# A convolution trunk in which two channel tiles of layer 1 change places, with one raw weight tile less and one general tile more

## The chip, the cores and the metric

The kernel runs on one core of a Trainium2 chip. The metric is the device time of one execution in microseconds; the median of three runs is quoted, and a profile of one execution is read beside it. Engines are named as in the profile: PE is the tensor engine, DVE the vector engine, ACT the scalar engine, POOL the GpSimd engine, and SP the queue from which all transfers are issued here.

## The reference

Two layers work on x of 2048 tokens by 1024 channels in float32. Each layer is `x + post_norm(mixer(pre_norm(x)))` with RMS norms. Layer 0 is a mixer of sliding-window attention and causal pooling. Layer 1, where the change lies, is a convolution module:

```
proj = h @ w_in                                  # 1024 x 3072
a, b, gate = split(proj, 3)
glu  = a * sigmoid(b)
conv = causal depthwise convolution of glu, 31 taps, + bias
mu, var = mean and variance of conv over all 1024 channels
cn = (conv - mu) * rsqrt(var + eps) * ln_g + ln_b
y  = silu(cn) * silu(gate)
out = y @ w_out
x  = x + rms_norm(out, post_norm)
```

The mean over all channels is what matters below: no part of `cn` can be formed before the convolution of each channel is there.

## The kernel before

Channels lie on the 128 partitions, so the 1024 channels are 8 tiles, numbered 0 to 7. Tokens are cut into two halves of 1024, and each half into two blocks of 512. A projection is 24 matmuls of 128x512 into one PSUM bank: 8 channel tiles k, and for each of them three matmuls, because every float32 operand is split in a high part and a low part: high weight by high input, high weight by low input, low weight by high input (`project`, L407). A weight tile is loaded raw, 512 KB, into a `wr` tile (`w_load`, L342). Then ACT copies its high part into `wh`, and DVE subtracts to get its low part `wl` (`w_split`, L373). For the weights `wc` of layer 1's input projection, the low part is formed once, kept in DRAM (`wcl`) and loaded from there. The raw tile is given back when both parts are there. The weights of the last block are different in one thing: their high and low parts are kept in general tiles `s4`, because this block is projected in two column parts of 256 (`last_block`, L1038), with matmuls of 128x256; there each weight is used for 24 matmuls and comes back for the second part.

Layer 1 runs in stages. For each half, `inproj1` (L1235) goes through the channel tiles in the order of `CONV_ORDER`; for each tile it projects b and a for both blocks. What comes next depends on the tile. Tiles 0, 1, 3, 5 and 7 are convolved on DVE (`conv_dve`, L1054): 29 multiply-add instructions of 128x1024, two starts and a sum, per half; the result goes to DRAM (`cd`). Tiles 2, 4 and 6 are convolved on PE (`conv_pe`, L1075) for both halves at once, when half 1's values are there: the values go to DRAM (`gt`), come back in another layout, are multiplied by Toeplitz tiles (`in_toep`) into the banks a0 and a1, and the results are stored in DRAM (`ct`) and loaded from there. After half 1's input projection come the gates (`gates1`, 16 projections), and while these run, `norms` (L1188) loads the convolved tiles of half 0, adds them up, takes their mean by a matmul with ones (`a0<-s4,ones`), the variance, and makes the mix: high and low parts for each tile k. Then `outproj` (L974) multiplies half 0's mix by the output weights (`in_wo`, eight projections for each block), and in this time the mix of half 1 is made. Half 1's first block is projected next, and its second block is the last block.

All instructions are issued through one helper, so the profile shows them on L189. The order in which they are issued is that of `Flow` (L54), a planner that runs when the program is built. PE's main line (the projections) goes on, and tasks with a priority (norms, convolutions, loads) are taken whenever, by its own cost estimates, their data are there and DVE and ACT are not more than `LAG` ahead of PE. Each engine then takes its instructions strictly in that order. SP's queue too is in that order. Tiles are taken from pools whose sizes are in `SLOTS` (L41); a task that finds its pool empty is not issued, and another goes ahead of it, so that a pool's size moves the whole order.

Of the kernel before, what the change touches and what calls it, by code (L numbers as in the profile page):

```python
# [34 lines left out]
DVE_CONV = (0, 1, 3, 5, 7)  # L35
PE_CONV = tuple(i for i in range(KT) if i not in DVE_CONV)
POOL_ORDER = (("u", 3), ("g", 3), ("u", 2), ("g", 2), ("u", 1), ("g", 1), ("u", 0), ("g", 0))
CONV_ORDER = (0, 1, 2, 3, 4, 5, 6, 7)

SLOTS = {  # L40
    "s4": 37, "t2": 5, "wr": 3, "wh": 2, "wl": 2, "xh": 2, "xr": 2, "ab": 1, "st": 3, "ms": 3, "rs": 2, "rh": 6,  # L41
    "mm": 4, "a0": 1, "a1": 1, "pt": 1, "pv": 1,
}
PACK = (
# [163 lines left out]
def trunk_kernel(tc, a):  # L208
# [49 lines left out]
    def grab(tag, cols=TH, dt=F32):  # L258
        flow.wait(lambda: avail[tag] > 0)
        return make(tag, cols, dt)  # L260

    def put(*tiles):
        for t in tiles:
            tag = owner.pop(t.name)
            at = 0.0
            for c in range(8):
                k = (t.name, c)
                at = max(at, flow.read.get(k, (0, 0))[0], flow.wrote.get(k, (0, 0))[0])
            freed[tag].append(at)
            freed[tag].sort()  # L270
            avail[tag] += 1
# [40 lines left out]
    wseq = []  # L312
# [2 lines left out]
        wseq += [("wa", 14 + g) if x == "g" else ("wu" if h else "wut", g) for x, g in POOL_ORDER]  # L315
        wseq += [("wo0", f) for b in range(NB) for f in range(KT)]
    for h in range(NH):
        wseq += [("wc", i) for c in CONV_ORDER for i in (8 + c, c)]
        wseq += [("wc", 16 + c) for c in range(KT)]
    for h in range(NH):  # L320
        wseq += [("wo1", f) for b in range(NB) for f in range(KT)]
# [79 lines left out]
    def take(name, i):  # L401
        flow.wait(lambda: wready)
        got = wready.pop(0)
        assert got[:2] == (name, i), (got[:2], name, i)
        return got[2:]

    def project(w, src, b, ready=None, part=slice(0, BL), order=tuple(range(KT)), tag="mm"):  # L407
        wh, wl = w
        bank = grab(tag)
        out = bank[:, :part.stop - part.start]  # L410
        for k in order:
            if ready is not None:
                flow.wait(lambda: ready(k, b))
            hi, lo = (t[:, part] for t in src(k, b))
            T.matmul(out, wh[:, k, :], hi, start=k == order[0], stop=False)
            T.matmul(out, wh[:, k, :], lo, start=False, stop=False)
            T.matmul(out, wl[:, k, :], hi, start=False, stop=k == order[-1])
            flow.pump()
        return bank, flow.t["P"]
# [86 lines left out]
    def pairs(tiles):  # L506
        return lambda k, b: halves(tiles[b][k])
# [604 lines left out]
    def tanh_of(bank, at, ths, b):  # L1112
        yield at
        th = yield from get("t2")
        A.activation(th, bank, AF.Tanh, scale=0.5)
        put(bank)
        ths[b] = th

    def glu(bank, at, ths, b, gv, n):
        yield at  # L1120
        yield from until(lambda: b in ths)
        th = ths[b]
        at = V.scalar_tensor_tensor(
            gv[:, b * PB:(b + 1) * PB, :], th.rearrange("f (p s) -> f p s", p=PB), 1.0,
            bank.rearrange("f (p s) -> f p s", p=PB), op0=ALU.add, op1=ALU.mult)
        put(th, bank)
        n[0] = at
        n[1] += 1

    def after_glu(half, i, gl, n, over):  # L1130
        yield from until(lambda: n[1] == NB)
        yield n[0]
        if i in DVE_CONV:
            slot = DVE_CONV.index(i)
            if half + 1 < NH:
                G.tensor_copy(gc[:, slot, :], gl[:, TH:])
            flow.spawn(conv_dve(half, i, slot, gl, over), 4)
        else:
            view = gt[i].rearrange("r x s -> (r x s)").rearrange("(c q s) -> c q s", c=P, q=PH)
            at = Q.dma_start(out=view[:, :, half * SG:(half + 1) * SG], in_=gl.rearrange("c (q s) -> c q s", q=PH))  # L1140
            put(gl)
            if half + 1 == NH:
                yield at
                flow.spawn(conv_pe(i, over), 2)
# [88 lines left out]
        stored.add((half, j, b))  # L1233

    def inproj1(half, hs, have, over):  # L1235
        for i in CONV_ORDER:
            ths, n = {}, [0.0, 0]
            w = take("wc", 8 + i)
            for b in range(NB):
                flow.spawn(tanh_of(*project(w, pairs(hs), b, lambda k, b: k in have[b]), ths, b), 0)  # L1240
            put(*w)
            dve = i in DVE_CONV
            gl = grab("s4", TH + HIST if dve else TH)
            if dve:
                G.tensor_copy(gl[:, :HIST], gc[:, DVE_CONV.index(i), :])
                gv = gl[:, HIST:].rearrange("f (s p) -> f p s", p=PH)
            else:
                gv = gl.rearrange("f (p s) -> f p s", p=PH)
            w = take("wc", i)
            for b in range(NB):  # L1250
                flow.spawn(glu(*project(w, pairs(hs), b), ths, b, gv, n), 0)
            put(*w)
            flow.spawn(after_glu(half, i, gl, n, over), 1)
# [26 lines left out]
    for half in range(NH):  # L1280
        inproj1(half, hs, have, over)
        now = hs
        hs, have = [{} for _ in range(NB)], [set() for _ in range(NB)]
        if half + 1 < NH:
            flow.spawn(prep(1, half + 1, hs, have, 2), 2)
        else:
            for h in range(NH):
                flow.spawn(norms(h, over, mixes[h], dones[h]), 1)
        gates1(half, now)
# [88 lines left out]
```

## Time and profile before

| what | value |
|---|---|
| median of three runs | 1494.03 us (1493.61 to 1494.33) |
| profiled execution | 1494.47 us |
| its span | 1492.7 us (1.8 us lie around it) |
| PE busy | 1464.9 us (98%), 7226 matmuls |
| DVE busy | 1220.6 us (82%) |
| ACT busy | 587.4 us (39%) |
| chain that ended last | PE 92%, DVE 3%, DMA 3% |

The profile's times start at the span's start. A row of the timeline is a run of like instructions: start, duration, engine, line, operation, out<-in, shape, count, and in brackets the idle time ahead of it with what ended it. Durations of matmuls in a run overlap, so the time of one is read from the distance of the starts. The chain that ended last follows the program back from its last instruction.

In layer 1, half 0's mean is taken at 1211.95 us, half 0's mix is projected from about 1282 us, half 1's mix from 1376.89 us (called X0 below: the first projection of its first block), and the last block from 1430.95 us.

### The profile page before, as it was taken

The page shows a single profiled execution, that of the slowest core. Times are in us where ns is not written, and L with a number is a line of the kernel's source. Part 1 is how long each engine was busy: PE and PEld are TensorE (multiplying, and loading weights), DVE is VectorE, ACT ScalarE, POOL GpSimd, SP SyncE. Part 2 cuts the span into 40 slices and gives each one's busy share as a digit, 9 for nine tenths or more (in the row PEclk, how much of TensorE's full clock was granted, in tenths as well). Part 3 has the DMA queues.
Part 4 walks back from the last instruction along what each step waited for, and adds up shares of the span by engine and source line. Part 5 has one row for each costly group of instructions (what it writes and reads, how often), then busy time and mean ns, then how long its engine had stood idle before and what let it go on. Part 6 is the DMA issues. An engine that isn't in the chain of part 4 may idle for free.

```text
span 1492.7 us, 19290 instructions
## 1 busy us (share of the span) xinstructions
PE 1464.9 (98%) x7226; PEld 1189.9 (80%) x7226; DVE 1220.6 (82%) x1903; ACT 587.4 (39%) x1093; POOL 48.6 (3%) x65
## 2 busy tenths in 40 slices
PE   8999999999999999999999999999999999999896
PEld 6877778788887778788888888888888878878696
DVE  7888877778888787576799999939999699789886
ACT  6454343555454434454211123211212135556541
POOL 0000010000000000000010000000000000000000
PEclk9999999999999999999999999999999999999998
DMA  6122144666551024356632446533654865734685
GB/s 226 60 81 70 66 141 138 197 229 222 187 173 50 29 85 166 106 180 221 202 114 94 132 127 209 186 127 118 214 187 154 273 197 197 242 127 141 213 280 184
DMA packets 121294, 236.78 MB, mean 159 GB/s; under 512 B 33776, under 2 KB 57968, under 8 KB 121200
## 3 DMA queue, kind: packets, MB, share of 16 engines
q1 hardware_dynamic: 121200, 235.55, 48.6%
q8 instruction: 57, 0.93, 0.3%
q14 instruction: 37, 0.30, 0.1%
HBM read 184.13 MB, written 51.38 MB: 158 GB/s over the span
## 4 chain that ended last, share of the span: by engine, by line
PE 92%; DVE 3%; DMA 3%; ACT 1%; issue 0%; SPq 0%; POOL 0%; POOLq 0%; ACTq 0%; DVEq 0%
PE mm L189 81%; PE a L189 5%; PE pv L189 3%; PE pt L189 2%; DVE s L189 2%; DMA s<-in_toep 2%; DMA s<-ct 1%; DVE wl L189 0%; ACT s L189 0%; ACT t L189 0%; DMA wr<-in_wa 0%; DVE t L189 0%; SPq L189 0%; ACT wh L189 0%; DMA ct<-t 0%
## 5 line engine op out<-in xcount | busy, mean ns | idle before, releaser
L189 PE MATMUL mm<-s,wh 128*128 128x512 f32 (+1 forms) x3616 | 1136.1, 395 | 12.4 <-ACT s L189 10.4
L189 PEld LDWEIGHTS mm<-s,wh 128*128 128x128 f32 x3616 | 669.1, 189 | 160.8 <-ACT s L189 11.6
L189 PE MATMUL mm<-s,wl 128*128 128x512 f32 (+1 forms) x1808 | 710.1, 393 | 0.0
L189 PEld LDWEIGHTS mm<-s,wl 128*128 128x128 f32 x1808 | 341.0, 189 | 76.4
L189 DVE SCALAR_TENSOR_TENSOR s<-s,packed,s 128x1024 f32<-128x1024 f32 x290 | 352.6, 1280 | 0.0
L189 ACT ACTIVATE wh<-wr 128x1024 fp32r<-128x1024 f32 (+1 forms) x138 | 145.3, 1053 | 394.1 <-PE mm L189 252.1
L189 DVE TENSOR_TENSOR wl<-wr,wh 128x1024 fp32r<-128x1024 f32 (+1 forms) x90 | 109.1, 1212 | 56.4 <-ACT wh L189 54.9
L189 DVE TENSOR_TENSOR s<-s,s 128x512 f32<-128x512 f32 (+4 forms) x124 | 114.2, 942 | 11.2 <-DMA s<-ct 4.3
L189 ACT ACTIVATE t<-mm 128x512 f32<-128x512 f32 (+1 forms) x122 | 68.6, 562 | 105.5 <-PE mm L189 105.5
L189 DVE TENSOR_TENSOR t<-t,t 128x512 f32<-128x512 f32 (+1 forms) x131 | 86.4, 664 | 16.5 <-ACT t L189 14.5
L189 PE MATMUL a<-s,s 128*128 128x128 f32 (+2 forms) x592 | 91.6, 292 | 3.0 <-DMA s<-in_toep 2.6
L189 PEld LDWEIGHTS a<-s,s 128*128 128x128 f32 x592 | 80.4, 190 | 13.5 <-DMA s<-in_toep 5.6
L189 ACT ACTIVATE s<-mm 128x512 f32<-128x512 f32 (+1 forms) x116 | 67.9, 585 | 52.9 <-PE mm L189 46.8
L189 DVE SCALAR_TENSOR_TENSOR s<-t,mm 128x512 f32<-128x512 f32 x48 | 40.2, 837 | 55.4 <-PE mm L189 51.3
L189 ACT ACTIVATE s<-t 128x512 fp32r<-128x512 f32 (+1 forms) x52 | 48.8, 942 | 53.2 <-DVE t L189 52.6
L189 ACT ACTIVATE t<-s 128x512 f32<-128x512 f32 x80 | 48.6, 628 | 51.2 <-DVE s L189 36.8
L189 DVE TENSOR_TENSOR t<-pt,packed 128x512 f32<-128x512 f32 x64 | 44.1, 689 | 23.6 <-PE pt L189 23.3
L189 DVE TENSOR_TENSOR s<-t,s 128x512 fp32r<-128x512 f32 (+1 forms) x56 | 52.5, 939 | 12.3 <-ACT s L189 11.5
L189 ACT ACTIVATE s<-s 128x512 fp32r<-128x512 f32 (+1 forms) x56 | 44.8, 813 | 32.3 <-DMA s<-in_wc 16.5
L189 ACT ACTIVATE s<-s,st 128x128 f32<-128x128 f32 x128 | 49.4, 388 | 12.2 <-DVE st L189 12.1
L189 POOL TENSOR_TENSOR rs<-ms,mhalf 128x4 f32<-128x4 f32 (+1 forms) x21 | 27.3, 1301 | 796.6 <-DVE ms L189 796.6
L189 DVE TENSOR_TENSOR s<-s,xr 128x512 f32<-128x512 f32 x56 | 37.8, 688 | 8.2 <-DMA xr<-in_xp 5.7
(100 smaller groups left out, 920.0 us busy)
## 6 DMA issues: line engine op xcount, KB each, us to landing
wr<-in_wo SPq DMA_DIRECT2D x64, 512.0 KB, 3.8
wr<-in_wc SPq DMA_DIRECT2D x48, 512.0 KB, 4.8
wl<-wcl SPq DMA_DIRECT2D x48, 512.0 KB, 3.4
wr<-in_wa SPq DMA_DIRECT2D x27, 512.0 KB, 4.2
s<-in_wc SPq DMA_DIRECT2D x24, 512.0 KB, 5.2
wcl<-s SPq DMA_DIRECT2D x24, 512.0 KB, 3.6
s<-in_toep SPq DMA_DIRECT2D x24, 384.0 KB, 5.0
xr<-in_xp SPq DMA_DIRECT2D x32, 256.0 KB, 4.5
```

The source lines that it names most:

```text
L189: fn(*args, **kw)
```

## The change

Two tables of numbers change. `SLOTS` gets one general tile `s4` more (37 to 38) and one raw weight tile `wr` less (3 to 2). `CONV_ORDER` becomes a pair with one order for each half, and in half 1 tile 7 comes before tile 6; the list of weights `wseq` (L318) and `inproj1` (L1235) take the order of the half.

```diff
-CONV_ORDER = (0, 1, 2, 3, 4, 5, 6, 7)
+CONV_ORDER = ((0, 1, 2, 3, 4, 5, 6, 7), (0, 1, 2, 3, 4, 5, 7, 6))

 SLOTS = {
-    "s4": 37, "t2": 5, "wr": 3, "wh": 2, "wl": 2, ...
+    "s4": 38, "t2": 5, "wr": 2, "wh": 2, "wl": 2, ...

     for h in range(NH):
-        wseq += [("wc", i) for c in CONV_ORDER for i in (8 + c, c)]
+        wseq += [("wc", i) for c in CONV_ORDER[h] for i in (8 + c, c)]

     def inproj1(half, hs, have, over):
-        for i in CONV_ORDER:
+        for i in CONV_ORDER[half]:
```

Because the planner looks at free tiles, the order changes in many places. Three are shown.

First, PE's queue from the last Toeplitz group of tile 6 (`a1`, six of its matmuls) to half 0's mean (`ones`); `mm` are projections, and the lines left out are whole or part projections of 128x512, three matmuls in each two rows. Before:

```order
L189 MATMUL a1_1532_9586<-s4_1499_9396,s4_1533_9587 128x128 x6
L189 MATMUL mm_1536_9615<-s4_1346_8084,wh_1505_9429 128x512 x2
L189 MATMUL mm_1536_9615<-s4_1346_8084,wl_1506_9430 128x512
...
L189 MATMUL mm_1548_9735<-s4_1276_7605,wh_1541_9667 128x512 x2
L189 MATMUL mm_1548_9735<-s4_1276_7605,wl_1542_9668 128x512
L189 MATMUL a0_1551_9744<-s4_1524_9552,ones_139 128x512
L189 MATMUL a1_1553_9749<-s4_1524_9552,ones_139 128x512
```

The same stretch of PE's queue now:

```order
L189 MATMUL a1_1555_9830<-s4_1525_9580,s4_1556_9831 128x128 x6
L189 MATMUL mm_1553_9815<-s4_1345_8082,wh_1534_9651 128x512 x2
L189 MATMUL mm_1553_9815<-s4_1345_8082,wl_1535_9652 128x512
...
L189 MATMUL mm_1565_9906<-s4_1330_7963,wh_1545_9759 128x512 x2
L189 MATMUL mm_1565_9906<-s4_1330_7963,wl_1546_9760 128x512
L189 MATMUL a0_1566_9921<-s4_1512_9501,ones_139 128x512
L189 MATMUL a1_1567_9923<-s4_1512_9501,ones_139 128x512
```

Between the last Toeplitz matmul and the mean stood 57 matmuls of projections (38 rows), and now there are 42 (28 rows); the mean itself stands some five projections later in the program.

Second, DVE's queue at X0, from the weight subtraction (`wl`) for the projection behind X0. The mix's low parts are the rows in which a tile `s4` is made from another and itself, with nothing else; the last one that X0 needs is the last row here. Before:

```order
L189 TENSOR_TENSOR wl_1787_11097<-wr_1758_10946,wh_1786_11096 128x1024
L189 TENSOR_TENSOR t2_1712_10725<-t2_1712_10725,t2_1788_11100 128x512
L189 TENSOR_TENSOR s4_1665_10467<-s4_1665_10467,t2_1747_10896 128x512
...
L189 SCALAR_TENSOR_TENSOR s4_1661_10440<-s4_1661_10440,packed_169,t2_1771_11026 128x512 x2
L189 TENSOR_SCALAR ms_1797_11154<-pt_1793_11141 128x4
...
L189 TENSOR_TENSOR s4_1799_11160<-s4_1656_10422,s4_1799_11160 128x512
L189 TENSOR_TENSOR s4_1801_11168<-s4_1665_10467,s4_1801_11168 128x512
```

DVE's queue from the like subtraction to the last low part that X0 needs, now:

```order
L189 TENSOR_TENSOR wl_1780_11074<-wr_1760_10971,wh_1779_11073 128x1024
...
L189 SCALAR_TENSOR_TENSOR s4_1640_10331<-s4_1640_10331,packed_169,t2_1765_10990 128x512
...
L189 TENSOR_TENSOR s4_1793_11133<-s4_1644_10363,s4_1793_11133 128x512
L189 TENSOR_TENSOR s4_1796_11139<-s4_1659_10440,s4_1796_11139 128x512
...
L189 TENSOR_TENSOR s4_1797_11152<-s4_1667_10490,s4_1797_11152 128x512
...
L189 TENSOR_TENSOR s4_1798_11161<-s4_1631_10292,s4_1798_11161 128x512
L189 TENSOR_TENSOR s4_1799_11164<-s4_1633_10296,s4_1799_11164 128x512
L189 TENSOR_TENSOR s4_1632_10294<-s4_1632_10294,s4_1794_11135 128x512
L189 TENSOR_TENSOR s4_1800_11167<-s4_1660_10453,s4_1800_11167 128x512
```

The weight's subtraction was followed by 14 rows to that last low part, and now by 25 rows; two low parts of the other block (`s4_1798` and `s4_1799`) and the work for them come before it.

Third, SP's queue at the start of the last block; `wr_1859` is the raw tile of its weight 3 before and of its weight 2 now, and `s4_1864` and `s4_1865` are loads of x. Before:

```order
L189 DMA wr_1859_11486<-in_wo1 128x1024
L189 DMA xr_1860_11496<-x1_0_0_104 128x512
L189 DMA out_y<-s4_1730_10819 128x512
L189 DMA xr_1861_11507<-x1_0_0_104 128x512
L189 DMA out_y<-s4_1730_10819 128x512
L189 DMA s4_1864_11519<-x1_1_1_107 128x4x256
L189 DMA s4_1865_11520<-x1_1_1_107 128x4x256
L189 DMA wr_1870_11543<-in_wo1 128x1024
```

SP's queue at the same place now:

```order
L189 DMA wr_1859_11489<-in_wo1 128x1024
L189 DMA xr_1860_11495<-x1_0_0_104 128x512
L189 DMA out_y<-s4_1730_10817 128x512
L189 DMA xr_1861_11510<-x1_0_1_105 128x512
L189 DMA out_y<-s4_1690_10609 128x512
L189 DMA s4_1864_11522<-x1_1_1_107 128x4x256
L189 DMA s4_1865_11523<-x1_1_1_107 128x4x256
L189 DMA wr_1870_11546<-in_wo1 128x1024
```

The rows stand alike, but each raw load here is for one weight earlier in the list than before.

## Rows read from the trace of the kernel before

**Rows 1.** The page, busy time of each engine (share of span) and its instructions.

```profile
PE 1464.9 (98%) x7226; PEld 1189.9 (80%) x7226; DVE 1220.6 (82%) x1903; ACT 587.4 (39%) x1093; POOL 48.6 (3%) x65
```

**Rows 2.** Waits of PE: engine line <- releaser: us in total, times, longest.

```profile
PE mm L189 <- ACT s L189: 10.4, 4, 5.7
PE a L189 <- DMA s<-in_toep: 2.6, 5, 0.9
```

**Rows 3.** Timeline of PE at X0: start, us, engine, operation, count [idle before].

```profile
1376.89 0.63 PE L189 MATMUL mm<-s,wh 128*128 128x512 f32 x2
...
1377.59 0.62 PE L189 MATMUL mm<-s,wh 128*128 128x512 f32 x2
...
1381.49 0.50 PE L189 MATMUL mm<-s,wh 128*128 128x512 f32 x1 [0.73 <-DVE s L189]
...
1386.72 0.79 PE L189 MATMUL mm<-s,wh 128*128 128x512 f32 x1 [3.71 <-ACT s L189]
1387.72 0.79 PE L189 MATMUL mm<-s,wh 128*128 128x512 f32 x1 [0.21 <-DVE s L189]
...
1388.74 1.05 PE L189 MATMUL mm<-s,wh 128*128 128x512 f32 x2
```

**Rows 4.** A stretch: length, busy PE PEld DVE ACT POOL, PEclk, DMA.

```profile
1375.00:1395.00 20.00, 15.35 (x57) 11.75 (x57) 18.27 (x31) 12.25 (x20) 1.48 (x1) 0.83 0.59 205
```

**Rows 5.** Timeline of DVE at X0.

```profile
1378.41 1.22 DVE L189 TENSOR_TENSOR wl<-wr,wh 128x1024 fp32r<-128x1024 f32 x1
...
1386.98 2.49 DVE L189 TENSOR_TENSOR s<-s,s 128x512 fp32r<-128x512 f32 x4
```

**Rows 6.** Chain that ended last, around half 0's mean: start, us, what.

```profile
1198.49 0.66 PE mm L189 x3
...
1199.69 2.49 DMA ct<-t
...
1202.27 8.31 DMA s<-ct
...
1210.67 1.24 DVE s L189
...
1211.95 1.98 PE a L189 x4
```

**Rows 7.** Transfers of the whole program: count, KB each, median us to landing.

```profile
wr<-in_wo SPq DMA_DIRECT2D x64, 512.0 KB, 3.8
...
s<-in_toep SPq DMA_DIRECT2D x24, 384.0 KB, 5.0
...
s<-ct SPq DMA_DIRECT2D x6, 512.0 KB, 7.6
```

**Rows 8.** Transfers issued from 1295 to 1300 us.

```profile
s<-ct SPq DMA_DIRECT2D x1, 512.0 KB, 6.6
```

**Rows 9.** Transfers issued from 1184 to 1199 us.

```profile
s<-ct SPq DMA_DIRECT2D x1, 512.0 KB, 10.8
s<-in_toep SPq DMA_DIRECT2D x1, 384.0 KB, 8.3
```

**Rows 10.** The page, groups of instructions: busy us, mean ns.

```profile
L189 DVE SCALAR_TENSOR_TENSOR s<-s,packed,s 128x1024 f32<-128x1024 f32 x290 | 352.6, 1280 | 0.0
...
L189 DVE TENSOR_TENSOR t<-t,t 128x512 f32<-128x512 f32 (+1 forms) x131 | 86.4, 664 | 16.5 <-ACT t L189 14.5
```

**Rows 11.** Timeline of PE in the last block.

```profile
1443.61 11.89 PE L189 MATMUL mm<-s,s 128*128 128x256 f32 x99
```

**Rows 12.** Timeline of ACT in the last block.

```profile
1443.24 1.06 ACT L189 ACTIVATE s<-wr 128x1024 fp32r<-128x1024 f32 x1 [0.80 <-DMA wr<-in_wo]
```

**Rows 13.** Transfers issued from 1420 to 1460 us.

```profile
wr<-in_wo SPq DMA_DIRECT2D x6, 512.0 KB, 5.8
```

**Rows 14.** Timeline of SP in the last block.

```profile
1427.74 0.33 SPq L189 DMA_DIRECT2D wr<-in_wo  x1
```

**Rows 15.** Timeline of DVE in the last block.

```profile
1432.01 1.23 DVE L189 TENSOR_TENSOR wl<-wr,wh 128x1024 fp32r<-128x1024 f32 x1 [1.17 <-ACT wh L189]
```

More of the change, by code (lines that the diff above doesn't have):

```diff
@@ L37 @@
 POOL_ORDER = (("u", 3), ("g", 3), ("u", 2), ("g", 2), ("u", 1), ("g", 1), ("u", 0), ("g", 0))
-CONV_ORDER = (0, 1, 2, 3, 4, 5, 6, 7)
+CONV_ORDER = ((0, 1, 2, 3, 4, 5, 6, 7), (0, 1, 2, 3, 4, 5, 7, 6))
 SLOTS = {
-    "s4": 37, "t2": 5, "wr": 3, "wh": 2, "wl": 2, "xh": 2, "xr": 2, "ab": 1, "st": 3, "ms": 3, "rs": 2, "rh": 6,
+    "s4": 38, "t2": 5, "wr": 2, "wh": 2, "wl": 2, "xh": 2, "xr": 2, "ab": 1, "st": 3, "ms": 3, "rs": 2, "rh": 6,
     "mm": 4, "a0": 1, "a1": 1, "pt": 1, "pv": 1,
```

## The prediction

> **What bounds the kernel now.** I read the page first: TensorE (PE) is busy 98% of the span [rows 1]. Its instructions are the same after the change, 4588 rows in the program's order in both, so the time can move only by what PE waits and by the clock that it is granted. Second the table of waits: PE's largest is on ScalarE (ACT), 10.4 us in 4 waits, the longest at the kernel's start; then 2.6 us on the Toeplitz tiles [rows 2]. There is little to win, and the question is which places that just fit now stop fitting. Third the timeline of the largest hole, at the first projection on half 1's mix (X0 below). PE waits 0.73, 3.71 and 0.21 us there, and then two matmuls take 1.05 us instead of 0.63 [rows 3]; the mean granted clock of 1375 to 1395 is 0.83, so PE came back from the wait at the lower of its two levels, 1.2 of 2.4 GHz [rows 4]. The waits are 4.65 us; a mean of 0.83 over 20 us is 6.8 us at the lower level, which costs at most 3.4, less where PE was waiting anyway. I put the hole at 7.5 us. DVE makes it: its weight subtraction for the projection behind X0 starts at 1378.41 and stands ahead of the last parts of the mix, whose last low part is the second of the four in the group at 1386.98 [rows 5].
>
> **What the change moves.** In half 1 of layer 1, tile 7 (convolved by VectorE, DVE, in 32 instructions) comes before tile 6 (convolved by PE). So tile 7's convolution starts sooner, and tile 6's, which serves both halves, ends nearer to half 0's channel mean. And weights are loaded into two raw tiles instead of three. In order of time:
>
> Term 1, half 0's mean. The mean's matmul needs all tiles, tile 6 last. From 1198.49, where PE's last Toeplitz group ends, ACT takes 1.2 us until the store at 1199.69, the store 2.49, the load 8.31, DVE's sum 1.24; the mean starts at 1211.95, 13.46 us later [rows 6]. Before, 57 matmuls of 0.23 us (three in the 0.70 from 1376.89 to 1377.59 [rows 3]) stand in between, 13.2 us, and PE waited 0.3. Now 42 do, 9.7 us. With the load at 8.31 the wait is 3.7, with the median of 7.6 [rows 7] 3.0, with 6.6 [rows 8] 2.0, with 10.8 [rows 9] 6.2. I take the median: 3.0 less the 0.3 of before is +2.7, bounds +1.7 and +5.9. It cannot be a gain, since the chain is the same and the cover shorter.
> The Trainium skill (DMA: Bandwidth & Descriptors, Anatomy of one DMA) fits a transfer as 2.0 us and its bytes at 436 GB/s, an estimate of 3.2 us for 512 KB; by it the chain is 8.3 us, the cover holds and this term is nothing. The row of 8.31 speaks against that fit here.
>
> Term 2, the Toeplitz tiles of tile 6. PE's five waits for such tiles cost 2.6 us, the longest 0.9 [rows 2]; landings are 5.0 as a median and 8.3 where traffic is dense [rows 7, 9]. They now stand in SP's queue behind stores of tile 7's result and of a gate. Bounds 0 and +1.5; I take +0.5, one average wait more.
>
> Term 3, the first projection on half 0's mix. From the mean to the last low part that it needs, DVE has 69 instructions, 43.7 us at 0.66 us for 512 columns and 1.2 for a weight [rows 5, 10]. Beside it PE has 177 matmuls of 0.23 us and twelve small ones, about 43 us. Before, PE had five projections more there, and no wait. The two now balance; DVE's own waits on the statistics come on top. Bounds 0 and +5; I take +1, nearer to the low end, since the trace of before has no wait there.
>
> Term 4, half 1's mean. The load of tile 6 for it is issued 32 matmuls (7.4 us) ahead, against 6.6 to 8.3 for the load and 1.24 for the sum [rows 6, 8]. Bounds 0 and +2; +0.5.
>
> Term 5, X0. The weight subtraction of the next projection cannot start before ACT has read its weight into a split tile that the projection ahead of X0 frees: 1.5 us into X0 (1376.89 and 1378.41 [rows 3, 5]). DVE takes its queue in order. Before, 14 rows stand from it to the last low part of the mix and take 9.8 us (1378.41 to 1388.2). Now 25 rows do, among them post-norm work of half 0 and parts of half 1's other block. At 0.62 us each (2.49 for four), a weight at 1.2 and the small ones at 0.16 this is 16.9 us. PE has the mix up to k = 2 and waits for the rest: +7.1. The end of DVE's queue sets this, not how far ahead DVE was. Bounds +4 (if the clock stays up between the shorter waits, 3.4 back) and +9 (if the lower level lasts 4 us longer). I take +7.
>
> Term 6, the last block. PE needs a weight each 2.88 us (24 of the 99 matmuls in 11.89 us [rows 11]). With three tiles the loads are already just in time: ACT waits 0.80 us for one [rows 12], and the median landing is 5.8 us [rows 13]. With two tiles the load of a weight can start only when the weight two before it has been split. Weight 3's then starts at 1433.2 (end of weight 1's subtraction, 1432.01 + 1.23) instead of 1427.74 [rows 14, 15]; it is ready 5.8 + 1.06 + 1.23 later, at 1441.3, and wanted at about 1440.6 (one weight and two small matmuls before the group of 99). From there two weights cost one load and one split, 8.1 us, against 5.8 of PE: 2.3 us late twice more, at weights 5 and 7. That is 0.7 + 4.6 = 5.3; with landings of 3.8, the median of all such loads [rows 7], it is +0.6, with 6.6 as in rows 8 some +8. As fewer loads will be in flight at once I take +4, bounds 0 and +8.
> The Trainium skill (Trainium Kernel Development and Optimization, Best Practices) advises to double-buffer; by it two tiles are enough, this term is nothing and the sum 4 us less. The 0.80 us that ACT waits even with three tiles speaks against it here.
>
> In the rest of the kernel two raw tiles stand against projections of 5.55 us (24 of 0.231), 11.1 us for two weights; load 3.8 [rows 7] and split 2.3 leave 5 us, so I put them at nothing. Where load and queueing reach 8.8 us that cover is gone (rival 3).
>
> Sum, on the profiled execution: 1494.47 + 2.7 + 0.5 + 1 + 0.5 + 7 + 4 = 1510.2 us. It stood 0.4 above the median of 1494.03, so 1509.7.
>
> **Rivals.**
> 1. Faster. Tile 7's convolution, 29 instructions of 1.22 us (352.6 us for 290 [rows 10]) and three more, some 38 us, leaves the stretch between half 0's mean and X0. If DVE is then so far ahead that half 1's mix is ready, X0's 7.5 us vanish; with term 1 at +2.7 and the rest at nothing the time is about 1489. It decides at X0: has DVE written the last low part when PE issues its first matmul there? Against it: the order puts 25 DVE rows behind a subtraction that PE's own progress releases.
> 2. No net change, about 1494. For it: loads at 6.6 leave term 1 at 1.7, the others may fit into what lies in between, and a partly filled X0 can give 2 us back. Against it: X0's loss rests on counted rows.
> 3. Two raw tiles starve PE in all of layer 1's output projection. If a load with its queueing takes 10 us, two weights take 12.3 us against 11.1, 0.6 each; for the 24 weights of 5.55 us ahead of the last block that is 14 more, about 1524. For it: ACT and DVE are taken in order, so a split can wait behind other work. Against it: the median of 3.8 [rows 7].
>
> **How the numbers follow.** Forecast 0.75, rival 1 0.10, rival 2 0.07, rival 3 0.08. The forecast's own range is 1500 (the terms near their low ends, +6) to 1518 (some of them near the high ends). To hold 8 in 10 it reaches to rival 2 below and toward rival 3 above: 1494 to 1520. A measurement of this kernel tells about 0.2%, 3 us, from no change. Faster is rival 1 less a part of it that ends within those 3 us, 0.09; same is rival 2 and that part, 0.08; slower is the forecast and rival 3, 0.83.
>
> **What would show it.** Term 1: a PE wait of 2 to 4 us on DVE before half 0's mean, behind a load of tile 6's result. Term 5: X0 some 20 us long instead of 13, with waits on ACT and DVE after k = 2 and the granted clock lower there. Term 6: PE waits on ACT or DVE at weights 3, 5 and 7 of the last block. Wrong: X0 at 5.6 us (rival 1), no PE wait in the last block (two tiles suffice), or waits in each projection of the output (rival 3).

## The result and the profile after

The changed kernel takes 1510.62 us (median of 4, 1508.13 to 1513.25) against 1493.82 us; the ratio is 1.0113, with a 95% interval of 1.0101 to 1.0125. The forecast was 1509.7 us. The sum came out within 1 us, but its terms did not all do so: one was nothing, two were larger than I had taken them, and it is luck that they made up for each other.

First the page's busy times and the granted clock in 40 slices of the profiled execution (span 1508.6 us, 15.9 us longer than before):

```profile
PE 1473.7 (98%) x7226; PEld 1192.1 (79%) x7226; DVE 1219.6 (81%) x1903; ACT 586.2 (39%) x1093; POOL 49.0 (3%) x65
...
PEclk9999999999999999999999999999999999998898
```

DVE and ACT are busy as long as before, and PE's busy time has grown by 8.8 us with the same 7226 matmuls [rows 1]: part of the loss is not waiting but matmuls that take longer, in the stretches with the lower clock and beside the waits. The waits of PE, in us, times and longest:

```profile
PE mm L189 <- ACT s L189: 9.3, 4, 5.6
PE mm L189 <- DVE s L189: 7.0, 11, 1.7
PE a L189 <- DMA s<-in_toep: 5.4, 6, 2.4
PE pv L189 <- DVE s L189: 3.0, 2, 1.9
```

Against [rows 2], the wait on ACT is not longer, but the Toeplitz tiles cost 2.8 us more, and there are now eleven waits of projections on DVE. Before there were four:

```profile
PE mm L189 <- DVE s L189: 2.0, 4, 0.7
```

To see where the time went, I laid the start of the same projection of the two timelines side by side. The difference grows like this:

| PE reaches | before | after | later by | added in this stretch |
|---|---|---|---|---|
| half 1 of layer 1, its 15th projection | 1052.36 | 1052.38 | 0.02 | 0 |
| first projection on half 0's mix | 1282.36 | 1285.08 | 2.72 | +2.7 (terms 1, 2) |
| X0 | 1376.89 | 1380.41 | 3.52 | +0.8 (terms 3, 4) |
| second projection behind X0 | 1397.04 | 1406.60 | 9.56 | +6.0 (term 5) |
| last block | 1430.95 | 1440.50 | 9.55 | 0 |
| its second column part | 1455.34 | 1472.01 | 16.67 | +7.1 (term 6) |
| end of the span | 1492.7 | 1508.6 | 15.9 | -0.8 |

**Half 0's mean.** The chain that ended last, around tile 6's convolution, answers to [rows 6]:

```profile
1205.84 7.69 DMA s<-in_toep
1213.54 0.04 issue
1213.58 1.60 PE a L189 x12
...
1233.49 1.60 PE a L189 x12
1235.09 9.69 PE mm L189 x42
1244.79 1.72 PE a L189 x4
```

A Toeplitz load of 7.69 us is on the chain, and PE waited 2.43 of it. But from the last Toeplitz group to the mean (1244.79) the chain runs through PE alone: 42 matmuls in 9.69 us as worked out, and no wait behind them. The load of tile 6 that the mean needs was issued at 1238.60, and landed in 4.5 us:

```profile
s<-ct SPq DMA_DIRECT2D x1, 512.0 KB, 4.5
```

When this load was issued, no other transfer was in flight; before, three were. DVE's sum ended at 1244.33 us and the mean's first matmul started at 1244.62, so the cover held by 0.3 us.

**X0.** PE's timeline (start, us, and in brackets the idle time before it) answers to [rows 3]:

```profile
1383.40 0.50 PE L189 MATMUL mm<-s,wh 128*128 128x512 f32 x1 [0.52 <-DVE s L189]
...
1385.21 1.17 PE L189 MATMUL pv<-s,onesr 128*128 128x512 f32 x2 [1.06 <-DVE s L189]
...
1390.63 0.80 PE L189 MATMUL mm<-s,wh 128*128 128x512 f32 x1 [2.75 <-ACT s L189]
1391.60 0.79 PE L189 MATMUL mm<-s,wh 128*128 128x512 f32 x1 [0.18 <-DVE s L189]
...
1395.22 0.80 PE L189 MATMUL mm<-s,wh 128*128 128x512 f32 x1 [0.69 <-DVE s L189]
...
1398.22 0.79 PE L189 MATMUL mm<-s,wh 128*128 128x512 f32 x1 [0.95 <-DVE s L189]
...
1399.24 1.05 PE L189 MATMUL mm<-s,wh 128*128 128x512 f32 x2
```

The projections wait twice more than before, and two matmuls of other work (`pv`) wait too. All waits here add up to 6.15 us against 4.65, which is only 1.5 of the 6.0 us; the rest is the two `pv` matmuls and matmuls that run slowly between the waits. The pair at 1399.24, the start of the next projection, is still slow (1.05 us for two). The row of the stretch answers to [rows 4]; the mean granted clock is 0.65 where it was 0.83:

```profile
1380.00:1400.00 20.00, 13.69 (x39) 8.78 (x38) 18.57 (x33) 12.77 (x19) 1.32 (x1) 0.65 0.44 159
```

DVE's timeline answers to [rows 5]:

```profile
1381.52 1.23 DVE L189 TENSOR_TENSOR wl<-wr,wh 128x1024 fp32r<-128x1024 f32 x1 [0.65 <-ACT wh L189]
...
1393.27 5.68 DVE L189 TENSOR_TENSOR s<-s,s 128x512 f32<-128x512 f32 x9
```

The subtraction starts at 1381.52, and the last low part that X0 needs is the eighth of the nine in the group at 1393.27; it ends at 1398.2, just before PE's last wait ends. That is 16.7 us for the 25 rows behind the subtraction and itself.

**The last block.** PE's timeline of its first column part, where [rows 11] had 99 matmuls in one piece:

```profile
1447.41 3.20 PE L189 MATMUL mm<-s,s 128*128 128x256 f32 x24
...
1452.45 3.11 PE L189 MATMUL mm<-s,s 128*128 128x256 f32 x24 [0.76 <-DVE s L189]
1455.85 6.13 PE L189 MATMUL mm<-s,s 128*128 128x256 f32 x48 [0.29 <-DVE s L189]
1462.73 3.36 PE L189 MATMUL mm<-s,s 128*128 128x256 f32 x24 [0.76 <-DVE s L189]
1467.78 4.39 PE L189 MATMUL mm<-s,s 128*128 128x256 f32 x22 [1.69 <-DVE s L189]
```

Waits of 3.5 us stand here, at weights 3, 4, 6 and 7 (each has 24 matmuls). They cost more than their idle time: that is counted from the recorded end of a matmul, and in an unbroken run the next one starts before it (0.12 us apart, at 0.28 us each). The last wait is followed by 22 matmuls that take 4.2 us from start to start instead of 2.7, most of them 0.21 each instead of 0.12, which is the lower clock again (0.81 as a mean of 1467 to 1476):

```profile
1467.00:1476.00 9.00, 8.22 (x57) 8.22 (x58) 5.52 (x12) 0.81 (x3) 1.02 (x1) 0.81 0.83 258
```

ACT waits for the raw weights, with up to 3.06 us where [rows 12] had 0.80:

```profile
1450.08 1.06 ACT L189 ACTIVATE s<-wr 128x1024 fp32r<-128x1024 f32 x1 [1.72 <-DMA wr<-in_wo]
...
1464.48 1.06 ACT L189 ACTIVATE s<-wr 128x1024 fp32r<-128x1024 f32 x1 [3.06 <-DMA wr<-in_wo]
```

The load of weight 7 shows the tile's way. SP's row of its issue, and DVE's rows of the subtractions of weights 5 and 7:

```profile
1458.34 0.33 SPq L189 DMA_DIRECT2D wr<-in_wo  x1
```

```profile
1457.09 1.23 DVE L189 TENSOR_TENSOR s<-wr,s 128x1024 fp32r<-128x1024 f32 x1 [0.53 <-ACT s L189]
...
1466.51 1.22 DVE L189 TENSOR_TENSOR s<-wr,s 128x1024 fp32r<-128x1024 f32 x1
```

The load is issued 0.02 us after weight 5's subtraction ends (1458.32), lands 6.1 us later, is read by ACT at 1464.48 and split at 1467.73, and PE goes on at 1467.78. The loads of weights 3 to 6 likewise start within 0.05 us of the end of the subtraction two weights before.

### The profile page after: what moved, and what is told of

The parts are those of the page before. It is cut to its first block, busy times and chain, and to the rows that moved or that the text cites. A ratio compares the mean times of both kernels' runs of the same rounds, so it can differ in the third digit from the quotient of the medians.

```text
span 1508.6 us, 19289 instructions
## 1 busy us (share of the span) xinstructions
PE 1473.7 (98%) x7226; PEld 1192.1 (79%) x7226; DVE 1219.6 (81%) x1903; ACT 586.2 (39%) x1093; POOL 49.0 (3%) x65
## 4 chain that ended last, share of the span: by engine, by line
PE 87%; DMA 6%; DVE 3%; issue 2%; ACT 2%; SPq 0%; POOLq 0%; DVEq 0%; ACTq 0%
PE mm L189 76%; PE a L189 5%; PE pv L189 3%; DVE s L189 3%; DMA s<-in_toep 2%; PE pt L189 2%; DMA gt<-s 1%; ACT s L189 1%; DMA xr<-x 1%; DMA wr<-in_wo 0%; DMA s<-ct 0%; SPq L189 0%; DVE wl L189 0%; ACT wh L189 0%; ACT t L189 0%
## 5 line engine op out<-in xcount | busy, mean ns | idle before, releaser
L189 PEld LDWEIGHTS mm<-s,wh 128*128 128x128 f32 x3616 | 669.1, 189 | 165.5 <-ACT s L189 12.3
L189 DVE TENSOR_TENSOR t<-t,t 128x512 f32<-128x512 f32 (+1 forms) x131 | 85.9, 663 | 17.7 <-ACT t L189 15.9
```

The lines of the kernel that those rows point to most:

```text
L189: fn(*args, **kw)
```

## The experiments

Theory: the parts of the change act at places of their own: the order of the tiles at the Toeplitz tiles, the pools' plan at X0, the missing raw tile in the last block. The rivals are with each run.

**The raw tile alone.** In `SLOTS` only `"wr": 3` becomes 2; the planner's order of DVE at X0 stays as it was.

```diff
-    "s4": 37, "t2": 5, "wr": 3, ...
+    "s4": 37, "t2": 5, "wr": 2, ...
```

> Before with one raw weight tile less and nothing else; DVE's queue at X0 is that of before, row for row. Theory (the raw tiles cost in the last block alone): the last block is some 7 us longer, with PE waits on DVE at weights 3, 5 and 7 of 3 to 4 us together and the lower clock behind the longest of them; X0 stays 13.1 us long; time 1493.8 + 7 = 1501, 1498 to 1503. Rival (two raw tiles starve PE in the whole output projection): waits from 1282 us on, +14, about 1508. Rival (the last block's loss in the changed kernel comes from the order of DVE and SP there, not from the tile): under 1 us, 1494 to 1495.

Measured: 1500.2 us, ratio to before 1.0054 (1.0041 to 1.0067). X0 with the projection behind it takes 19.4 us (20.2 before), and the first part of the last block 32.3 us instead of 24.4. PE's timeline there:

```profile
1439.95 0.50 PE L189 MATMUL mm<-s,s 128*128 128x256 f32 x2 [1.63 <-ACT s L189]
...
1441.38 0.58 PE L189 MATMUL mm<-s,s 128*128 128x256 f32 x1 [0.93 <-DVE s L189]
...
1454.04 3.10 PE L189 MATMUL mm<-s,s 128*128 128x256 f32 x24 [0.59 <-DVE s L189]
...
1458.30 2.86 PE L189 MATMUL mm<-s,s 128*128 128x256 f32 x22 [1.16 <-DVE s L189]
```

These waits, 4.3 us in all, are at weights 3, 6 and 7, a little more than the theory's 3 to 4 us and not at its places. Nothing between 1282 and 1430 us waits but X0. So the raw tile's price is paid in the last block alone, and it is paid with DVE's and SP's old order too; both rivals fall.

**The order of the tiles alone.** `CONV_ORDER` and its two uses as in the change, `SLOTS` as before.

```diff
-CONV_ORDER = (0, 1, 2, 3, 4, 5, 6, 7)
+CONV_ORDER = ((0, 1, 2, 3, 4, 5, 6, 7), (0, 1, 2, 3, 4, 5, 7, 6))
```

> Before with the order 7 6 in half 1 and nothing else. DVE has 18 rows, 11.1 us by their durations, from the weight subtraction to the last low part at X0, against 15 rows and 10.1 us before and 26 rows and 17.4 us in the changed kernel. Theory (each part of the change has its own place): the stretch up to half 0's mix loses 2 to 4 us at the Toeplitz tiles, X0 1 us, the last block nothing: 1497 to 1499. Rival (the new order of the tiles makes the changed kernel's loss at X0, the pool's sizes only the last block): X0 near 19 us, about 1503. Rival (the order alone costs nothing, its Toeplitz waits come from the pools): 1494.

Measured: 1496.39 us, ratio 1.0024 (1.0015 to 1.0033), a little under the range. The Toeplitz waits in its page of waits are

```profile
PE a L189 <- DMA s<-in_toep: 4.6, 5, 2.1
```

2.0 us over [rows 2]. PE reaches half 0's mix 1.8 us later than before. X0 with its neighbour takes 20.8 us, 0.6 more than before, and the first part of the last block 25.3 instead of 24.4, where the theory had nothing. So the order alone costs mainly what it does at the Toeplitz tiles; it does not make X0's loss.

**The pools alone.** 38 and 2 tiles, the old order of tiles.

```diff
-    "s4": 37, "t2": 5, "wr": 3, ...
+    "s4": 38, "t2": 5, "wr": 2, ...
```

> Before with 38 general and 2 raw tiles, old order of tiles. DVE has 5 rows, 4.5 us, from the weight subtraction to the last low part at X0. Theory: X0 falls from 13.1 to some 6.5 us and the lower clock there goes, -7 to -8; the last block pays +7 for the raw tile; nothing at the Toeplitz tiles: 1493 to 1495. Rival (X0's length is set by how late the mix starts, not by the rows behind the weight subtraction): X0 stays near 13, 1500 to 1502.

Measured: 1491.4 us, ratio 0.9991 (0.9982 to 0.9999), a little under the range: the general tile gives at X0 a little more than the raw tile costs. X0 has no wait at all, and the two projections take 11.5 us. The row of 1376 to 1389 us shows PE busy throughout, at the full clock:

```profile
1376.00:1389.00 13.00, 12.90 (x56) 10.19 (x55) 13.00 (x21) 10.37 (x16) 0.00 (x0) 1.00 0.82 276
```

The last block's first part is 30.7 us. So the pools' plan can close X0 or open it; it depends on what rows the planner puts behind the weight subtraction. The changed kernel has the same pools and the other order of tiles, and there the plan opened it.

**A third raw tile for the last block of the changed kernel.** Weights 2 and 5 of the last block are loaded into general tiles.

```diff
-            raw = yield from get("wr")
+            if n >= len(wseq) - 8 and n % 3 == len(wseq) % 3:
+                raw = (yield from get("s4")).rearrange("p (k f) -> p k f", k=KT)
+            else:
+                raw = yield from get("wr")
```

> The changed kernel, where weights 2 and 5 of the last block are loaded into general tiles, so that three raw loads can be in flight there again; all before the last block is as in the changed kernel. Theory (the last block waits for the raw tile): the waits at weights 3, 5 and 7 and the lower clock there go, -6 to -7.5, 1503 to 1505. Rival (loads slow each other, so a third in flight gains nothing, or the splits are late by ACT's and DVE's order): 1508 to 1511.

Measured: 1502.75 us, ratio 1.0069 (1.0057 to 1.0082), just under the range. The first part takes 24.4 us, as long as before the change, and PE waits for nothing in it:

```profile
1438.00:1462.00 24.00, 24.00 (x201) 23.73 (x200) 20.29 (x32) 13.55 (x24) 1.32 (x1) 1.00 0.82 284
```

X0 stays as it was, 26.2 us with its neighbour. This settles term 6: it was 7.1 us and all of it is the number of raw loads that can be in flight.

**Both together, without the order of tiles.** The pools alone, with the edit above.

> The old order of tiles with 38 general and 2 raw tiles, as in the run with the slots alone, and weights 2 and 5 of the last block loaded into general tiles. Theory (each term in its own place): the gain at X0 stays, 8 to 9 us, and the last block is 24.4 us long as before instead of 30.6: 1491.4 - 6.2 = 1485, 1483 to 1487, faster than both kernels. Rival (general tiles are short there, the third load takes one from the mix): waits elsewhere in the last block, 1488 to 1492.

Measured: 1485.33 us, ratio 0.9952 (0.9939 to 0.9966), faster than both kernels by some 7 and 25 us. X0 has no wait, and neither has the first part of the last block:

```profile
1376.00:1388.00 12.00, 11.91 (x52) 9.36 (x51) 12.00 (x19) 9.52 (x16) 0.00 (x0) 1.00 0.80 272
1422.00:1447.00 25.00, 25.00 (x209) 24.74 (x208) 21.43 (x33) 13.99 (x26) 1.01 (x1) 1.00 0.85 280
```

**X0 of the changed kernel with fewer rows in between.** Five tasks at a time, not three, make the first mix of half 1.

```diff
-            yield from spread_tasks([apply(...) for k in range(KT)], 3, 1 + b + 2 * half)
+            yield from spread_tasks([apply(...) for k in range(KT)], 5 if half and not b else 3, 1 + b + 2 * half)
```

> The changed kernel, where five tasks instead of three at a time make the first mix of half 1: DVE has 19 rows, 12.3 us, from the weight subtraction to the last low part at X0, instead of 26 rows and 17.4 us; all up to half 1's mean is as in the changed kernel. Theory (those rows set X0): X0 and the projection behind it take, like the others, their rows' time and 9 us more, 21.5 instead of 26.2: -4 to -5, about 1506. Rival (the mix is late by its own chain of DVE, ACT and loads, whatever stands between): -1 or nothing, 1509 to 1511.

Measured: 1507.46 us, from 1501.43 to 1508.55 in four runs, ratio 1.0090 (1.0072 to 1.0108). That interval overlaps the changed kernel's, so the time alone doesn't decide. The trace, which is of the fastest of the four, does for X0: the two projections take 20.5 us instead of 26.2, with these waits:

```profile
1382.88 0.50 PE L189 MATMUL mm<-s,wh 128*128 128x512 f32 x1 [1.82 <-ACT s L189]
...
1384.17 0.50 PE L189 MATMUL mm<-s,wh 128*128 128x512 f32 x1 [0.79 <-DVE s L189]
...
1387.97 0.79 PE L189 MATMUL mm<-s,wh 128*128 128x512 f32 x1 [1.12 <-ACT s L189]
...
1389.18 0.79 PE L189 MATMUL mm<-s,wh 128*128 128x512 f32 x1 [0.42 <-DVE s L189]
```

Over the kernels, the rows' time d behind the subtraction and the length L of the two projections go together: d 4.5, L 11.5; 7.8, 18.3 (below); 10.1, 20.2 and 19.4; 11.1, 20.8; 12.3, 20.5; 17.4, 26.2. My rule of L = d + 9 holds to some 2 us. Between 10 and 12 us of rows L hardly moves, and at the short end 11.1 is the least that PE needs.

**More traffic at the mean's load.** Four transfers of 512 KB that nothing reads, ahead of the load of tile 6.

```diff
+                if half == 0 and n == KT - 1:
+                    for e in range(4):
+                        nc.sync.dma_start(out=spare[e], in_=a["wc"][e])
```

> The changed kernel with four more transfers of 512 KB, DRAM to DRAM, issued ahead of half 0's load of tile 6, the one that its mean waits for; nothing else moves, and nothing reads them. Theory (that load lands in 4.5 us because there is little other traffic, and the cover of 42 matmuls is then 0.4 us more than its chain): it lands in 8 us or more, and the mean waits 2.5 to 4 us. Rival (the load is as long as its small pieces make it, alone or not): 4.5 to 5.5 us and a wait of at most 1.

Measured, in one execution: 1517.29 us. The chain that ended last:

```profile
1239.51 8.87 DMA s<-ct
...
1248.39 1.24 DVE s L189
...
1249.77 3.63 PE a L189 x4
```

The load takes 8.87 us instead of 4.5, and the mean waits 4.78 us, more than the theory's 2.5 to 4. Some 0.7 us of the wait is SP's: it issues the four transfers first, and so the load 4.2 us after the last Toeplitz group instead of 3.5. The four matmuls behind the wait take 3.63 instead of 1.72 us. The cover of 42 matmuls was enough only because the load met little else. The other traces say the same: in the six where this load is issued with nothing else in flight, the changed kernel's two among them, it takes 4.4 to 4.6 us, and in the four with the old order of tiles, where three transfers are in flight, 7.9 to 8.3.

**A third Toeplitz tile ahead for tile 6.**

```diff
-                while len(tts) < 2 and nt[0] < GPT // 2:
+                while len(tts) < (3 if i == 6 else 2) and nt[0] < GPT // 2:
```

> The changed kernel with three instead of two Toeplitz tiles loaded ahead for tile 6; this moves the planner, so that DVE has 10 rows, 7.8 us, from the weight subtraction to the last low part at X0. Theory: the waits for tile 6's Toeplitz tiles fall from 2.9 us to under 1.5, X0 and the projection behind it take 17 us instead of 26.2, the last block stays 31 us: 1498 to 1501. Rival (a third load only slows the other two under this traffic): the Toeplitz waits stay at 2.5 to 3 us, 1501 to 1503.

Measured: 1500.65 us, ratio 1.0050 (1.0037 to 1.0064). The time is in my theory's range, but not for its reason. X0 gave 7.9 us (18.3 instead of 26.2; the theory had 17), while tile 6's Toeplitz waits stayed at 2.65 us, as the rival had it:

```profile
1200.59 2.92 PE L189 MATMUL a<-s,s 128*128 128x128 f32 x24 [0.84 <-DMA s<-in_toep]
...
1213.61 2.11 PE L189 MATMUL a<-s,s 128*128 128x128 f32 x12 [1.81 <-DMA s<-in_toep]
```

**No loads of convolved tiles beside the Toeplitz loads.** Half 0's mean begins to load only when all eight tiles are there.

```diff
-        yield from until(lambda: len(over[half]) >= 5 and (half == 0 or gated))
+        yield from until(lambda: len(over[half]) >= (8 if half == 0 else 5) and (half == 0 or gated))
```

> The changed kernel, where half 0's mean starts to load its tiles only when all eight are there, so that none of the seven loads of convolved tiles (512 KB each) falls between the Toeplitz loads of tile 6. What comes later moves much (the mean's sum is then later by 8 loads and 7 sums), so only the stretch from 1185 to 1240 us is read. Theory (the waits for tile 6's Toeplitz tiles come from these loads beside them): Toeplitz landings of 5 us or less there and waits of under 0.8 us in all, against 2.9 in the changed kernel's profile. Rival (their own queueing behind weights and stores on SP makes them late): waits of 2 us or more.

Measured, in one execution: 1517.03 us, which the later mean explains: its mix is late for the output projection, where the longest wait on it is 8.80 us. In the stretch that was to be read, the waits are

```profile
1200.77 1.60 PE L189 MATMUL a<-s,s 128*128 128x128 f32 x12 [1.79 <-DMA s<-in_toep]
...
1216.59 1.60 PE L189 MATMUL a<-s,s 128*128 128x128 f32 x12 [0.34 <-DMA s<-in_toep]
```

2.1 us in all; the median landing from 1185 to 1240 us is 5.8 us against 6.6 in the changed kernel. The theory falls: these loads are not what makes most of the Toeplitz waits. Its rival has the size right, but nothing here shows that SP's queue is the reason.

**The changed kernel once more.**

> The changed kernel once more, to see how far its waits repeat. Theory (X0 and the last block are set by the order and by loads that hardly vary, the Toeplitz tiles by traffic that does): X0 with the projection behind it 26 us and the last block 31 us again within 1 us, the Toeplitz waits anywhere from 1 to 5 us. Rival (all of the loss varies alike): X0 or the last block off by over 1.5 us.

Measured, in one execution: 1510.83 us. X0 with its neighbour is 26.4 us again. The first part of the last block is 29.8 us, 1.7 less than in the first profile, since the lower clock behind its last wait is not there this time (a mean of 1.00 in the row below). So this part varies more than I had said, by as much as the rival asked for, and X0 does not. The Toeplitz waits are 5.7 us, against 5.4 in the first profile, a little above the 1 to 5 that I gave.

```profile
1381.00:1401.00 20.00, 13.27 (x39) 8.36 (x38) 18.63 (x32) 13.11 (x20) 1.32 (x1) 0.66 0.43 158
1441.00:1471.00 30.00, 25.95 (x203) 24.46 (x202) 22.52 (x35) 13.67 (x24) 1.01 (x1) 1.00 0.82 268
```

## Why the prediction was right, and where its terms were not

The forecast case is the one that took place. Term by term:

- Term 1, half 0's mean (+2.7): wrong, it was nothing. The failed step is "I take the median": the load's 7.6 us belonged to loads that stood among others, as in [rows 6]. With the mean five projections later those others had gone by, and it took 4.5 us, less than any row I had bounded it with. The cover was rightly counted at 9.7 us, and it held by only 0.3. The Trainium skill (DMA: Bandwidth & Descriptors, Anatomy of one DMA) gives its fit for transfers that GpSimd issues, and these are issued from SP, which the prediction did not say. Taken as an estimate for them all the same, 3.2 us for these bytes, it gave the right answer here, no wait, and I had set it aside on the strength of one row under traffic. It is still 1.3 us short of this load (4.5 us), and 5.7 us short of the same load among four others (8.87 us).
- Term 2, the Toeplitz tiles (+0.5): mis-sized, 2.8 us of waits in all, over its upper bound of 1.5. The order alone makes 2.0 of them. For tile 6 by itself, which the term was about, the waits are 0.6 to 1.0 us in the four runs with the old order of tiles and 2.1 to 3.3 in the eight with the new one, whatever the pools. Loads of convolved tiles beside them are not the reason, and a third tile ahead does not cure it; why those loads are late is open. Also open: at tile 2's store ahead of such loads (`gt`) the two profiles of the changed kernel show 8.1 and 7.8 us, and two kernels with the same order there (a third raw tile; five tasks) 6.7 and 6.3; the chain to the first Toeplitz wait, 1.2 us, goes through that store.
- Terms 3 and 4 (+1 and +0.5): small as said; waits of 0.22 and 0.34 us, and 0.8 us in the table.
- Term 5, X0 (+7): right in mechanism, 6.0 us. The rows took 16.7 us, as worked out (16.9). The rest: the subtraction started 1.1 us into X0 and not 1.5. Before, it stood behind DVE's own rows ([rows 5] has no idle time ahead of it) and not, as the prediction has it, behind ACT; now it waits 0.65 us for ACT. And PE used the parts of the mix one by one, so that only the last remained when DVE was done, where before two were left.
- Term 6, the last block (+4): right in mechanism, mis-sized, 7.1 us in this profile and 5.4 in the other. The waits came at weights 3, 4, 6 and 7 and not at 3, 5 and 7, so that the account of which load is late is only roughly right. The step that failed is "as fewer loads will be in flight at once I take +4": the working itself gave 5.3 by the median landing, and I took it down without a row for that. Landings were 3.5 to 7.3 us. What the working left out is the lower clock behind the longest wait, 4.2 - 2.7 = 1.5 us. The Trainium skill's advice to double-buffer (Trainium Kernel Development and Optimization, Best Practices) names no depth; read as the prediction read it, that two tiles are enough and this term is nothing, it does not hold here: two tiles cost 7.9 us by themselves, and a third in flight took the cost away.

Of the rivals, the first has its truth in another kernel: with the same pools and the old order of tiles X0 does close, for 8.7 us over the two projections. The point from which it decides was the one named, whether the mix is there when PE arrives; and it was not tile 7's earlier convolution that decided it but the planner's rows. Rival 3 is excluded by the run with the raw tile alone.

## What to carry to other kernels

Where a planner sets the order, a pool's size can matter more through the order that follows than through the tile itself: count, on the engine that runs late, the rows between what the previous stage releases and what the next one needs. Size a load by what else is on its way at that moment, not by its median over the program. And give a stage that uses up its two tiles faster than one load and one split (5.8 us against 8.1 here) its own depth of buffers, borrowing tiles that are free there.

## What the runs showed that I had not expected

Short waits can cost more than themselves. At the mean with added traffic, a wait of 4.78 us was followed by four matmuls in 3.63 us instead of 1.72. In the last block, a wait of 1.69 us was followed by 22 matmuls in 4.2 us instead of 2.7, and in the other profile of the same kernel, behind 1.27 us, the same 22 took 2.7. The wait's length alone does not decide it: ahead of the same 22 matmuls, 1.59 us in the run with added traffic was followed by the lower clock (0.60 as the mean clock of 4.3 us from the wait's end), and 1.58 us in the run with the pools alone was not (1.00). In the stretch of X0, with its several waits, the clock was 0.65 and 0.66 in two profiles. What decides it between such waits these runs don't tell.
